# Mixer of a two-layer hybrid encoder on one core: the order of TensorE's products, from the inverses' transposes to w_out, left to a scheduler or written as a list

## The chip, the cores and the metric

One core of a Trainium2 chip. The metric is the device time of one execution in microseconds (us), as the median of several runs; the profile is of one execution more.

## The reference, cut to what matters

Two layers of the following, on 256 tokens of width 1024, all in float32:

```python
x = x + 0.5 * _swiglu(_rmsnorm(x, ffn1_norm[i]), ...)
proj = _rmsnorm(x, mix_norm[i]) @ w_in[i]
q, k, v, z, beta_logit, alpha, hy_in = jnp.split(proj, IN_SPLITS, axis=-1)
o_dn = _deltanet_group(q, k, v, z, beta_logit, alpha, ...)   # both directions
o_hy = _hyena_group(hy_in, ...)                               # two long convolutions
x = x + jnp.concatenate([o_dn, o_hy], axis=-1) @ w_out[i]
x = x + 0.5 * _swiglu(_rmsnorm(x, ffn2_norm[i]), ...)
```

The DeltaNet group is the gated delta rule, run forwards and backwards over the tokens, 4 heads of 128. Per chunk it solves a unit triangular system `a_mat`, then applies the state. The Hyena group takes v, x1, x2 from a short convolution and computes `z = x1 * (conv(v) + skip * v)`, then `z = x2 * (conv(z) + skip * z)`, with long convolutions by Fourier transform, and a norm.

## The kernel before

Activations lie with channels on the partitions (128) and the 256 tokens along the free axis. A large product is a loop over eight blocks of 128 channels. The half steps (SwiGLU) and w_out use weights split in two parts, three products for one; the projections that this change touches use plain float32 weights, 8 products (`pw`) for a chunk of 128 columns, each 128x256 and two instructions long. In this stretch lie the chunks h1 (gate of the first long convolution), v, h2 (gate of the second) and z (the delta rule's gate), four chunks each.

The delta rule's triangular systems, 16 of 128x128 (4 heads, 2 blocks of tokens, 2 directions; four systems make a quarter `q_`), are inverted in place by blocks. VectorE (DVE) makes the 16x16 diagonal blocks into `S`. Then, quarter by quarter: `stp` transposes S into `ST` (ScalarE, ACT, copies it); the step 16 is `pz` (to `zt`, by ACT) and `pp` (subtracted on DVE), 64 columns wide; the steps 32 and 64 are `pzq` (to `zq`, by ACT) and `ppq` (back to S on DVE and to ST on ACT), on 32x32 and 64x64 tiles of the array. Then the solve: `ph` products of S, ST, Mf and Mb with the right-hand sides `rho` (v's transposes `pv`, scaled), scaled to `uf`, `gv` or copied to `ub`; `po` is the output, normed to `on`, transposed back (`pot`), gated to `og`.

The Hyena side: `long_conv` makes `ze` and `zo` (even and odd part of a transform, ACT copies zo to `zq`), ten element-wise operations on DVE and GpSimd, and the inverse transform `py` (512 columns; for the second convolution `py2`, 128 columns). `pt` are h1's transposes to tokens. `acc` are w_out's 192 products, 24 for each of its eight row blocks: four of the Hyena half (blocks 4 to 7, from `yn`), four of the delta rule's (0 to 3, from `og`).

All engines take their instructions from queues in a fixed order. Before, a scheduler sets it at build time, by readiness in its own model and by priorities: each `stage(...)` (lvl, v, h1, quad, lc1, h2, z, hn, hw, solve, o, ow) raises its instructions by an offset. No order is written. PE's instructions thus mix: the delta rule's steps, which wait for each other through ACT and DVE, have pw, py and acc products between. PSUM tiles are two to each of the tags a, b, c, d, so a product waits for the reader of the tile before last.

Of the kernel before, what the change touches and what calls it, by code (L numbers as in the profile page):

```python
# [10 lines left out]
F32 = mybir.dt.float32  # L11
# [62 lines left out]
 'hold': 3,  # L74
 'ej': 0,
# [14 lines left out]
def trunk_kernel(ctx: ExitStack, tc: tile.TileContext, xt, ffn, wba, win, wout, par, fpar, fwo, fnorm, con, feat, wnd, out):  # L90
# [25 lines left out]

    def mm(o, l, r, start=True, stop=True, **kw):
        PE.matmul(o, lhsT=l, rhs=r, start=start, stop=stop, **kw)  # L118
# [202 lines left out]
    def proj32(o, w, ys):  # L321
        for k in range(KD):
            mm(o, w[:, k * 128:(k + 1) * 128], ys[k], start=(k == 0), stop=(k == KD - 1))
# [12 lines left out]
    def rank(acc, w, h, first, last):  # L336

        for m in range(KD):
# [168 lines left out]
    def mixer(l, ys, norm, ab, wcols):  # L507
# [100 lines left out]
        for a in range(2):  # L608
            PE.transpose(pba[:, a], bt[:, a * 128:(a + 1) * 128], ident[0:16, 0:16])
# [214 lines left out]
        def acols(t):  # L824
            return t.rearrange("p m (g b c) -> p m g b c", b=2, c=16)[:, :, :, 0]

        def bcols(t):
            return t.rearrange("p m (g b c) -> p m g b c", b=2, c=16)[:, :, :, 1]


        for q_ in range(4):
            qs = slice(4 * q_, 4 * q_ + 4)
            pz = psum("a", "pz", (128, 4, 4, 16))
            sta, sa, sb = acols(ST[:, qs]), S[:, qs], bcols(S[:, qs])
            for h in range(4):
# [35 lines left out]
        gt = tok("gt", 2)  # L871
        to_tokens(h1, gt)
        z1 = tok("zt", 2)
        for p in range(2):
            py = psum("c", "py", (128, CW))
            mm(py, dft(4 + p), u[p][0], stop=False)
            mm(py, dft(6 + p), u[p][1], start=False)
            V.tensor_tensor(out=z1[p], in0=py, in1=gt[p], op=ALU.mult)
        stage("quad")

        for n in (32, 64):
            for q_ in range(4):
                qs = slice(4 * q_, 4 * q_ + 4)
                pz = psum("a", "pzq", (128, 4, n))
                pp = psum("d", "ppq", (128, 4, n))
                zq = mx.tile([128, 4, n], F32, tag=f"zq{n}", name="zq", bufs=(2 if n == 32 else 1))
                for o in range(0, 128, 2 * n):
                    a, b = slice(o, o + n), slice(o + n, o + 2 * n)
                    for h in range(4):
                        mm(pz[b, h], XX[q_][a, h, b], ST[a, 4 * q_ + h, a])  # L890
                    A.activation(out=zq[b], in_=pz[b], func=AF.Copy)
                    if n == 32 or q_ < 2:
                        for h in range(4):
                            mm(pp[a, h], zq[b, h], S[b, 4 * q_ + h, b])
                        V.tensor_scalar(out=S[a, qs, b], in0=pp[a], scalar1=-1.0, scalar2=None, op0=ALU.mult)
                    if n == 32 or q_ >= 2:
                        for h in range(4):
                            mm(pp[b, h], S[b, 4 * q_ + h, b], zq[b, h])
                        A.activation(out=ST[b, qs, a], in_=pp[b], func=AF.Copy, scale=-1.0)

        stage("lc1")
        u = long_conv(z1, ab[1])

        stage("h2")

        x2 = []
        for i in range(4):
            t = ap_.tile([128, T], F32, tag="hc", name="x2", bufs=4)
            hconv(20 + i, 2, i, t)
            x2.append(t)  # L910
        stage("z")

        zs = []
        for i in range(4):
            t = mx.tile([128, T], F32, tag="zs", name="zs", bufs=4)
            chunk(24 + i, t, AF.Silu)
            zs.append(t)

        stage("hn")
        hn = Norm(4, CW, "b")  # L920
        for i in range(4):
            c = slice(i * 128, (i + 1) * 128)
            py = psum("c", "py2", (128, 2, 128))
            for p in range(2):
                mm(py[:, p], u[p][0][:, c], dft(4 + p), stop=False)
                mm(py[:, p], u[p][1][:, c], dft(6 + p), start=False)
            xv = x2[i].rearrange("c (t p) -> c p t", p=2)
            V.tensor_tensor(out=xv, in0=py, in1=xv, op=ALU.mult)
            hn.add(x2[i])
        hn.finish()  # L930

        stage("hw")

        acc = accumulators("ccdd")
        for i in range(4):
            t = ap_.tile([128, T], F32, tag="t1", name="yn", bufs=7)
            V.scalar_tensor_tensor(out=t, in0=x2[i], scalar=P[:, C_HYN + i:C_HYN + i + 1], in1=hn.rb, op0=ALU.mult, op1=ALU.mult)
            if 28 + i not in PRM["split"]:
                rank32(acc, load_raw(wout[l, 4 + i]), t, i == 0, False)
            else:  # L940
                with pr("feedw"):
                    w = load_w(wout[l, 4 + i])
                rank(acc, w, split_act(t, "y", 8), i == 0, False)
# [17 lines left out]
        uf, ub = [None, None], [None, None]  # L961
        gv1 = tt("gv1", rho[1], gbc(1, 1), ALU.mult)
        uf[0] = tt("uf0", heads("a", lambda h: S[:, 0 + h], rho[0]), gbc(0, 0), ALU.mult)
        p = heads("a", lambda h: ST[:, 12 + h], gv1)
        ub[1] = d2("ub1")
        A.activation(out=ub[1], in_=p, func=AF.Copy)
        p = heads("a", lambda h: Mf[:, h], uf[0])
        V.tensor_tensor(out=rho[1], in0=rho[1], in1=p, op=ALU.subtract)
        p = heads("a", lambda h: Mb[:, h], ub[1])
        V.tensor_tensor(out=rho[0], in0=rho[0], in1=p, op=ALU.subtract)  # L970
        gv0 = tt("gv0", rho[0], gbc(0, 1), ALU.mult)
        uf[1] = tt("uf1", heads("a", lambda h: S[:, 4 + h], rho[1]), gbc(1, 0), ALU.mult)
        p = heads("a", lambda h: ST[:, 8 + h], gv0)
        ub[0] = d2("ub0")
        A.activation(out=ub[0], in_=p, func=AF.Copy)

        stage("o")

        on = []
        for i in range(2):  # L980
# [11 lines left out]
            on.append(tt("on", po, bh(f), ALU.mult))  # L992
        stage("ow")
        for h in range(4):
            pt = psum("b", "pot", (128, T))
            for i in range(2):
                PE.transpose(pt[:, i * 128:(i + 1) * 128], on[i][:, h], ident)
            t = ap_.tile([128, T], F32, tag="t1", name="og", bufs=7)
            V.scalar_tensor_tensor(out=t, in0=pt, scalar=P[:, C_DNN:C_DNN + 1], in1=zs[h], op0=ALU.mult, op1=ALU.mult)
            if 32 + h not in PRM["split"]:  # L1000
                rank32(acc, load_raw(wout[l, h]), t, False, h == 3)
# [147 lines left out]
```

## Time and profile before

| | us |
| --- | --- |
| median of 3 runs | 1250.51 (1249.68 to 1251.75) |
| profiled execution | 1253.56 |
| its span, first to last instruction | 1251.8 |
| PE busy in it | 1210.9 |
| DVE busy | 875.5 |
| ACT busy | 588.8 |

The span is what the trace shows; the time of an execution is a little longer. The mean granted clock of PE over the span is 0.982 of full speed. A product's row counts from its start to its end, and products overlap a little, so in a dense run the distance of two starts is the price of the first.

### The profile page before, as it was taken

Reading aid. Unit: us, or ns where it says so; the run is one execution under the profiler, and the core shown is the slowest. Engines: PE = TensorE matmul, PEld = TensorE weight load, DVE = VectorE, ACT = ScalarE, POOL = GpSimd, SP = SyncE. Lnnn points to the kernel's source line nnn. Section 1 sums busy time; section 2 is a strip of 40 time slices with the busy share of each in tenths; the row PEclk is TensorE's granted clock in tenths of the full one; section 3 lists DMA queues with packets and bytes.
Section 4 is the critical chain, followed back from the end, with each engine's and each line's share of the span. In section 5 each row is a group of like instructions: output and inputs, shape, how many; then the busy total and the mean of one; then the engine's idle time right before and its main releaser. Section 6 shows DMA issues by size and latency. Waiting matters only on the chain.

```text
span 1251.8 us, 20519 instructions
## 1 busy us (share of the span) xinstructions
PE 1210.9 (97%) x7908; PEld 1063.9 (85%) x7908; DVE 875.5 (70%) x1483; ACT 588.8 (47%) x1058; POOL 306.8 (25%) x254
## 2 busy tenths in 40 slices
PE   6999989999999999999999999999999999999997
PEld 5888878978779899998888888888887898999996
DVE  6866677659954666667777767776597656766665
ACT  5544455362323445555554445553432334555553
POOL 5122233211221521113221214430202314111111
PEclk9999999999998899999999999999999988999998
DMA  8555667123222445556645556650231414455551
GB/s 292 172 168 192 195 204 228 31 68 101 69 74 96 135 135 188 190 188 204 210 127 188 181 168 210 222 169 16 77 111 51 136 60 143 156 186 188 193 186 53
DMA packets 53913, 186.36 MB, mean 149 GB/s; under 512 B 6157, under 2 KB 7088, under 8 KB 53816
## 3 DMA queue, kind: packets, MB, share of 16 engines
q1 hardware_dynamic: 50156, 179.01, 43.9%
q10 hardware_dynamic: 3660, 6.05, 1.6%
q8 instruction: 62, 1.02, 0.3%
q14 instruction: 35, 0.29, 0.1%
HBM read 183.98 MB, written 1.05 MB: 148 GB/s over the span
## 4 chain that ended last, share of the span: by engine, by line
PE 71%; DVE 13%; DMA 8%; ACT 3%; issue 3%; POOL 1%; DVEq 0%; SPq 0%; ACTq 0%
PE acc L118 18%; PE g L118 15%; PE u L118 14%; PE pw L118 10%; DMA raw<-in_win 6%; DVE wl L182 4%; DMA raw<-in_ffn 2%; PE py L118 1%; ACT wh L179 1%; PE pe L118 1%; PE pp L118 1%; PE ppq L118 1%; PE ph L118 1%; PE st L118 1%; DVE vs L552 1%
## 5 line engine op out<-in xcount | busy, mean ns | idle before, releaser
L182 DVE TENSOR_TENSOR wl<-raw,wh 128x1024 fp32r<-128x1024 f32 (+1 forms) x270 | 341.4, 1267 | 84.8 <-ACT wh L179 81.2
L179 ACT ACTIVATE wh<-raw 128x1024 fp32r<-128x1024 f32 (+1 forms) x270 | 282.1, 1048 | 121.0 <-PE acc L118 76.0
L118 PE MATMUL acc<-hp,wh 128*128 128x256 f32 x1408 | 265.9, 282 | 0.0
L118 PE MATMUL g<-yp,wh 128*128 128x512 f32 x656 | 245.0, 407 | 8.6 <-DVE yp L157 8.6
L118 PE MATMUL u<-yp,wh 128*128 128x512 f32 x656 | 236.0, 395 | 0.5 <-DVE ub L333 0.3
L118 PEld LDWEIGHTS acc<-hp,wh 128*128 128x128 f32 x1408 | 227.4, 190 | 3.6 <-issue 0.8
L368 POOL TENSOR_TENSOR sr<-gb,rb 128x256 f32<-128x256 f32 x88 | 110.4, 1254 | 450.7 <-ACT gb L366 450.7
L118 PE MATMUL acc<-hp,wl 128*128 128x256 f32 x704 | 194.3, 284 | 8.7 <-DVE wl L182 8.7
L118 PE MATMUL u<-yp,wl 128*128 128x256 f32 x656 | 168.9, 278 | 2.9 <-DVE wl L182 2.9
L118 PE MATMUL g<-yp,wl 128*128 128x256 f32 x656 | 171.7, 282 | 0.0
L118 PEld LDWEIGHTS g<-yp,wh 128*128 128x128 f32 x656 | 124.2, 189 | 40.6 <-DVE yp L157 9.7
L118 PE MATMUL pw<-y,raw 128*128 128x256 f32 x640 | 148.6, 381 | 0.0
L118 PEld LDWEIGHTS acc<-hp,wl 128*128 128x128 f32 x704 | 133.3, 190 | 13.0 <-DVE wl L182 11.1
L118 PEld LDWEIGHTS u<-yp,wh 128*128 128x128 f32 x656 | 123.2, 188 | 22.6 <-PE g L118 0.6
L118 PEld LDWEIGHTS pw<-y,raw 128*128 128x128 f32 x640 | 120.1, 190 | 25.9 <-issue 11.5
L118 PEld LDWEIGHTS u<-yp,wl 128*128 128x128 f32 x656 | 122.9, 188 | 11.3 <-DVE wl L182 4.3
L118 PEld LDWEIGHTS g<-yp,wl 128*128 128x128 f32 x656 | 124.6, 191 | 5.2 <-issue 1.4
L182 POOL TENSOR_TENSOR early<-raw,early 128x512 fp32r<-128x512 f32 (+1 forms) x44 | 75.5, 1729 | 93.9 <-ACT early L179 93.9
L332 ACT ACTIVATE gb<-g 128x256 f32<-128x256 f32 x88 | 33.4, 380 | 120.7 <-PE g L118 117.7
L153 DVE TENSOR_TENSOR hp<-ub,hp 128x256 fp32r<-128x256 f32 x88 | 56.8, 645 | 26.8 <-ACT hp L152 26.6
L333 DVE TENSOR_TENSOR gb<-g,gb 128x256 f32<-128x256 f32 x88 | 37.0, 420 | 44.3 <-ACT gb L332 44.3
L333 DVE TENSOR_TENSOR ub<-u,ub 128x256 f32<-128x256 f32 x88 | 37.0, 420 | 38.4 <-ACT ub L332 38.4
(436 smaller groups left out, 1669.8 us busy)
## 6 DMA issues: line engine op xcount, KB each, us to landing
raw<-in_ffn SPq DMA_DIRECT2D x264, 512.0 KB, 3.9
raw<-in_win SPq DMA_DIRECT2D x56, 512.0 KB, 4.5
raw<-in_wout SPq DMA_DIRECT2D x16, 512.0 KB, 3.9
w<-in_wnd ACTq DMA_DIRECT2D x16, 256.0 KB, 4.4
wo<-in_fwo ACTq DMA_DIRECT2D x8, 130.0 KB
X<-in_xt SPq DMA_DIRECT2D x4, 256.0 KB, 7.5
con_s<-in_con SPq DMA_DIRECT2D x1, 544.0 KB, 9.2
out<-X SPq DMA_DIRECT2D x2, 256.0 KB, 2.5
```

The costliest lines, as they stand in the source:

```text
L118: PE.matmul(o, lhsT=l, rhs=r, start=start, stop=stop, **kw)
L153: eng.tensor_tensor(out=lo, in0=src, in1=hi.bitcast(F32), op=ALU.subtract)
L179: op = A.activation(out=h, in_=raw[:, c], func=AF.Copy)
L182: eng.tensor_tensor(out=l_, in0=raw[:, c], in1=h.bitcast(F32), op=ALU.subtract)
L332: A.activation(out=t, in_=o[:, 1], func=AF.Copy)
L333: V.tensor_tensor(out=t, in0=o[:, 0], in1=t, op=ALU.add)
L368: G.tensor_tensor(out=sr, in0=sg, in1=norm.rb, op=ALU.mult)
L552: i = V.scalar_tensor_tensor(out=dst[:, lo:hi], in0=raw[:, lo + s_:hi + s_], scalar=P[:, w0 + j:w0 + j + 1], in1=dst[:, lo:hi], op0=ALU.mu ...
```

## The change

From `stp` to the last product of w_out, each product and transpose is put behind the one before it on PE (`in_line`: an order without a semaphore, on the same engine). The order is a list in the source: tuples are steps, numbers are gaps, filled with pw products of h2 and z from the generator `bulk()` until the gap's microseconds, at 0.43 a product, are used up. `"h2"` draws products until h2 is done, 99 all that are left. What stands ahead of the list in the source, the chunks of v and h1 and the transposes pv, is not in the line; the scheduler places it. Within the list the priorities are 800 ("delta") and 300 ("hyena").

With it go: all w_out products stand at the end, Hyena's first block, then pot, then the rest; `zq` of the steps 32 and 64 share two buffers (`zqd`), and a step's products for S and ST alternate head by head; pot and all ph use PSUM tag a; the second gate, its norm's sums and the norm are three steps (`py2_`, `st_`, `hn_`). The quarters run as 0, 3, 1, 2.

```diff
+ 'gap_b': 0.4, 'hyena': 300,
+ 'gap_l': 0.9, 'gap_q': 0.5, 'gap_s': 0.6, 'gap_o': 0, 'delta': 800,
...
+    def in_line(i):
+
+        if line[0]:
+            if line[1] is not None:
+                behind(i, line[1])
+            line[1] = i
+
     def mm(o, l, r, start=True, stop=True, **kw):
-        PE.matmul(o, lhsT=l, rhs=r, start=start, stop=stop, **kw)
+        in_line(PE.matmul(o, lhsT=l, rhs=r, start=start, stop=stop, **kw))
...
-        stage("lvl")
-        for q_ in range(4):
-            qs = slice(4 * q_, 4 * q_ + 4)
-            p = psum("a", "stp")
-            for h in range(4):
-                PE.transpose(p[:, h], S[:, 4 * q_ + h], ident)
-            A.activation(out=ST[:, qs], in_=p, func=AF.Copy)
...
+        def stp(q_):
+            p = psum("a", "stp")
+            for h in range(4):
+                transpose(p[:, h], S[:, 4 * q_ + h], ident)
+            A.activation(out=ST[:, quarter(q_)], in_=p, func=AF.Copy)
...
+            for k in range(KD):
+                proj32(p, w, yn, (k,))
+                if k < KD - 1:
+                    yield 0.43
...
+        def lc1_():
+            got["u"] = long_conv(got["z1"], ab[1])
...
+        def bulk():
+            for f_, *a in [(h2_, 0), (h2_, 1), (h2_, 2), (h2_, 3), (z_, 0), (z_, 1), (z_, 2), (z_, 3)]:
+                yield from f_(*a)
...
+        a_, b_, c_, d_ = 0, 3, 1, 2
+        L, Q, W = PRM["gap_l"], PRM["gap_q"], PRM["gap_s"]
+        line[:] = [True, None]
+        rest = bulk()
+        for x in [PRM["gap_b"], (stp, a_), (stp, b_), L, (pz16, a_, 0), (stp, c_), (pz16, b_, 1), (pp16, a_), (stp, d_), (pz16, c_, 0), (pp16, b_),
+                  (pz16, d_, 1), (pp16, c_), (tokens_,), (pzq, 32, a_), (pp16, d_), (pzq, 32, b_), Q, (ppq, 32, a_), (py_, 0), (pzq, 32, c_),
+                  (ppq, 32, b_), (py_, 1), (pzq, 32, d_), (ppq, 32, c_), Q, (pzq, 64, a_), (ppq, 32, d_), 2 * Q, (lc1_,), (pzq, 64, b_), (ppq, 64, a_), Q, (pzq, 64, c_),
+                  (ppq, 64, b_), Q, (fwd, 0), (pzq, 64, d_), (bwd, 1), (ppq, 64, c_), Q, (ppq, 64, d_), W, (less, 1), W, (less, 0), W, (fwd, 1), 2 * W, (bwd, 0), 2 * W,
+                  (po_, 1), (po_, 0), "h2", (py2_, 0), (py2_, 1), (py2_, 2), (py2_, 3), 2 * W, (st_,), 3 * W, (hn_,), 99, (wo_, 4, True), (og_,), (wo_, 5),
+                  (wo_, 6), (wo_, 7), (wo_, 0), (wo_, 1), (wo_, 2), (wo_, 3, False, True)]:
```

What this does to the engines' rows, at three places of layer 0. First PE, from the transposes stp on, before (x8 at stp are two quarters; pw are products of the projections):

```order
L822 MATMUL stp<-con_s,S 128x128 x8
L118 MATMUL pw<-y_2422,raw 128x256 x3
L118 MATMUL zo<-zt,con_s 128x512
L118 MATMUL pw<-y_2417,raw 128x256 x4
L118 MATMUL pw<-y_2422,raw 128x256 x2
L822 MATMUL stp<-con_s,S 128x128 x8
L118 MATMUL pw<-y_2422,raw 128x256 x2
L118 MATMUL pw<-y_2417,raw 128x256
L859 MATMUL pv<-con_s,vs 128x128 x2
L118 MATMUL pw<-y_2417,raw 128x256
L859 MATMUL pv<-con_s,vs 128x128 x2
L118 MATMUL pw<-y_2417,raw 128x256 x2
```

The same place with the change:

```order
L132 MATMUL stp<-con_s,S 128x128 x8
L129 MATMUL zo<-zt,con_s 128x512
L129 MATMUL pw<-y_2417,raw 128x256 x3
L129 MATMUL pz<-ST,xm 128x64 x4
L132 MATMUL stp<-con_s,S 128x128 x4
L132 MATMUL pv<-con_s,vs 128x128 x4
L129 MATMUL pz<-ST,xm 128x64 x4
L129 MATMUL pp<-S,zt_0_79 128x64 x4
L129 MATMUL pp<-zt_0_79,S 128x64 x4
L132 MATMUL stp<-con_s,S 128x128 x4
L129 MATMUL pz<-ST,xm 128x64 x4
```

The pw products between stp and the first pz became three, pz follows at once, and the four transposes pv stand in one group between the second stp and the second pz.

Second, ACT at the same place, before (raw and h are the evacuation and the middle tap of the last h1 chunk):

```order
L823 ACTIVATE ST<-stp 128x512 x2
L530 ACTIVATE raw__3355<-pw 128x256
L540 ACTIVATE h_3351<-raw__3355,par_s 128x256
L470 ACTIVATE zq<-zo 128x512
L853 ACTIVATE vs<-vs 128x256 x4
L823 ACTIVATE ST<-stp 128x512 x2
```

And with the change:

```order
L544 ACTIVATE raw__3263<-pw 128x256
L554 ACTIVATE h_3259<-raw__3263,par_s 128x256
L873 ACTIVATE ST<-stp 128x512 x2
L484 ACTIVATE zq<-zo 128x512
L837 ACTIVATE vs<-vs 128x256 x4
L882 ACTIVATE zt_0_79<-pz 128x16x16
```

The last h1 chunk's copy now stands ahead of the two copies to ST instead of behind them.

Third, PE where the steps of 32 begin, before (py is the inverse transform of the first long convolution; ze begins the second):

```order
L118 MATMUL pzq<-ST,xf 32x32 x4
L118 MATMUL pp<-S,zt_1_80 128x64
L118 MATMUL pp<-zt_1_80,S 128x64 x4
L118 MATMUL py<-t,con_s 128x512
L118 MATMUL py<-ab,con_s 128x512
L118 MATMUL ze<-zt,con_s 128x512
L118 MATMUL pw<-y_2422,raw 128x256 x2
L118 MATMUL ppq<-S,zq 32x32 x4
```

And with the change (the rows of ppq alternate from here, sixteen in all, and the first py stands behind them):

```order
L132 MATMUL pt<-con_s,h_3259 128x128
L129 MATMUL pzq<-ST,xf 32x32 x8
L129 MATMUL pp<-S,zt_1_80 128x64 x4
L129 MATMUL pp<-zt_1_80,S 128x64 x4
L129 MATMUL pzq<-ST,ex 32x32 x8
L129 MATMUL pw<-y_2422,raw 128x256 x2
L129 MATMUL ppq<-S,zqd 32x32
L129 MATMUL ppq<-zqd,S 32x32
```

The py products, which stood ahead of the first ppq, now come behind it, and two pw products stand between pzq and ppq.

## Rows read from the trace of the kernel before

**Rows 1.** The page: busy us of each engine, share, instructions.
```profile
PE 1210.9 (97%) x7908; PEld 1063.9 (85%) x7908; DVE 875.5 (70%) x1483; ACT 588.8 (47%) x1058; POOL 306.8 (25%) x254
```

**Rows 2.** What PE waits for: us, times, longest.
```profile
PE pot L997 <- DVE on L955: 2.4, 2, 1.3
...
PE zo L118 <- DVE zq L476: 1.3, 2, 0.6
...
PE acc L118 <- ACT yp L152: 1.2, 2, 0.7
...
PE pt L572 <- DVE rho L861: 1.1, 2, 0.5
...
PE acc L118 <- DVE yp L153: 1.0, 2, 0.6
...
PE ppq L118 <- ACT zq L891: 0.9, 2, 0.5
...
PE pot L997 <- DVE og L999: 0.9, 2, 0.5
```

**Rows 3.** Window, layer 0's stretch: PE, PEld, DVE, ACT, POOL busy, PEclk, DMA.
```profile
313.20:434.70 121.50, 117.17 (x889) 101.50 (x887) 81.66 (x136) 42.74 (x91) 33.84 (x23) 0.93 0.29 96
```

**Rows 4.** Timeline, PE, layer 0: start, duration, count.
```profile
334.08 1.06 PE L118 MATMUL pp<-zt,S 128*128 128x64 f32 x8
...
336.76 1.95 PE L118 MATMUL pz<-ST,xm 128*128 128x64 f32 x16
...
339.06 1.02 PE L118 MATMUL py<-er,con_s 128*128 128x512 f32 x2
...
342.60 0.43 PE L118 MATMUL pzq<-ST,xf 32*32 32x32 f32 x8
...
348.55 2.02 PE L118 MATMUL py<-t,con_s 128*128 128x512 f32 x2
...
358.70 0.69 PE L118 MATMUL ppq<-zq,S 32*32 32x32 f32 x16
...
359.32 1.12 PE L118 MATMUL ze<-zt,con_s 128*128 128x512 f32 x2
```

**Rows 5.** Windows of layer 0, columns as in rows 3.
```profile
333.30:338.50 5.20, 5.20 (x49) 5.20 (x48) 5.17 (x8) 0.38 (x1) 1.78 (x1) 1.00 0.33 101
...
344.20:347.50 3.30, 3.30 (x39) 3.08 (x39) 0.75 (x2) 0.63 (x3) 0.00 (x0) 1.00 0.00 0
...
347.60:351.00 3.40, 3.40 (x9) 2.07 (x9) 0.75 (x2) 0.00 (x0) 0.00 (x0) 0.50 0.00 0
...
385.20:388.50 3.30, 2.83 (x42) 2.56 (x38) 0.94 (x3) 1.70 (x5) 0.72 (x1) 1.00 0.03 5
...
388.60:395.30 6.70, 6.70 (x37) 6.24 (x38) 2.38 (x7) 1.95 (x6) 0.71 (x1) 0.50 0.00 0
...
415.80:419.20 3.40, 1.59 (x9) 0.69 (x7) 2.35 (x4) 2.10 (x3) 0.59 (x1) 1.00 0.80 280
...
419.30:426.00 6.70, 5.97 (x26) 5.68 (x27) 6.70 (x7) 2.94 (x8) 6.70 (x4) 0.50 0.56 172
```

**Rows 6.** Timeline, PE, around the first transposes of layer 0.
```profile
314.08 2.32 PE L118 MATMUL pw<-y,raw 128*128 128x256 f32 x10
...
316.24 1.04 PE L822 MATMUL stp<-con_s,S 128*128 128x128 f32 x8
...
319.21 1.12 PE L118 MATMUL zo<-zt,con_s 128*128 128x512 f32 x2 [0.64 <-DVE zq L476]
```

**Rows 7.** Timeline, ACT, the same place.
```profile
321.22 0.38 ACT L530 ACTIVATE raw__3355<-pw 128x256 f32<-128x256 f32 x1 [3.27 <-DVE h L552]
...
321.64 0.60 ACT L540 ACTIVATE h<-raw__3355,par_s 128x256 f32<-128x256 f32 x1
...
324.32 1.60 ACT L853 ACTIVATE vs<-vs 128x256 f32<-128x256 f32 x4 [1.60 <-DVE vs L552]
```

**Rows 8.** Timeline, DVE, the last tap of vs.
```profile
325.00 0.47 DVE L552 SCALAR_TENSOR_TENSOR vs<-raw__3270,par_s,vs 128x254 f32<-128x254 f32 x1
```

More of the change, by code (lines that the diff above doesn't have):

```diff
@@ L319, in load_raw, with proj32 @@
         return raw
-    def proj32(o, w, ys):
-        for k in range(KD):
+    def proj32(o, w, ys, ks=range(KD)):
+        for k in ks:
             mm(o, w[:, k * 128:(k + 1) * 128], ys[k], start=(k == 0), stop=(k == KD - 1))
@@ L334, in joined, with rank @@
         return t
-    def rank(acc, w, h, first, last):
-        for m in range(KD):
+    def rank(acc, w, h, first, last, ms=range(KD)):
+        for m in ms:
             for i, (a, b) in enumerate(((0, 0), (1, 0), (0, 1))):
@@ L870, in mixer @@
             h1.append(t)
[L871 to L943, printed above, removed]
@@ new lines, in pz16, with pp16 @@
+        def pz16(q_, n):
+            sta = acols(ST[:, quarter(q_)])
+            pz = psum("a", "pz", (128, 4, 4, 16))
+            for h in range(4):
+                mm(pz[:, h], xm[q_][:, h], sta[:, h])
+            zts[q_] = zt16[n % 2]
+            A.activation(out=acols(zts[q_]), in_=pz, func=AF.Copy)
+        def pp16(q_):
+            qs = quarter(q_)
+            sta, sa, sb, zt = acols(ST[:, qs]), S[:, qs], bcols(S[:, qs]), zts[q_]
+            pp = psum("d", "pp", (128, 2, 4, 4, 16))
+            for h in range(4):
+                mm(pp[:, 0, h], zt[:, h], sb[:, h])
+            for h in range(4):
+                mm(pp[:, 1, h], sa[:, h], acols(zt)[:, h])
+            V.tensor_tensor(out=sb, in0=sb, in1=pp[:, 0], op=ALU.subtract)
+            V.tensor_tensor(out=sta, in0=sta, in1=pp[:, 1], op=ALU.subtract)
@@ new lines, in halves, with pzq @@
+        def halves(n):
+            return [(slice(o, o + n), slice(o + n, o + 2 * n)) for o in range(0, 128, 2 * n)]
+        def pzq(n, q_):
+            pz = psum("a", "pzq", (128, 4, n))
+            zq = zqs[q_] = mx.tile([128, 256], F32, tag="zq", name="zqd", bufs=2)[:, 0:4 * n].rearrange("p (h c) -> p h c", h=4)
+            for a, b in halves(n):
+                for h in range(4):
+                    mm(pz[b, h], XX[q_][a, h, b], ST[a, 4 * q_ + h, a])
+            for a, b in halves(n):
+                A.activation(out=zq[b], in_=pz[b], func=AF.Copy)
@@ new lines, in ppq @@
+        def ppq(n, q_):
+            pp = psum("d", "ppq", (128, 4, n))
+            zq, qs = zqs[q_], quarter(q_)
+            to_s, to_st = n == 32 or q_ < 2, n == 32 or q_ >= 2
+            for a, b in halves(n):
+                for h in range(4):
+                    if to_s:
+                        mm(pp[a, h], zq[b, h], S[b, 4 * q_ + h, b])
+                    if to_st:
+                        mm(pp[b, h], S[b, 4 * q_ + h, b], zq[b, h])
+            for a, b in halves(n):
+                if to_s:
+                    V.tensor_scalar(out=S[a, qs, b], in0=pp[a], scalar1=-1.0, scalar2=None, op0=ALU.mult)
+                if to_st:
+                    A.activation(out=ST[b, qs, a], in_=pp[b], func=AF.Copy, scale=-1.0)
@@ L959, in gbc, with fwd, bwd, less @@
             return bh(gam[:, a, d])
[L961 to L980, printed above, removed]
+        uf, ub, on = [None, None], [None, None], [None, None]
+        def fwd(j):
+            uf[j] = tt("uf", heads(lambda h: S[:, 4 * j + h], rho[j]), gbc(j, 0), ALU.mult)
+        def bwd(j, g_):
+            p = heads(lambda h: ST[:, 8 + 4 * j + h], g_)
+            ub[j] = d2("ub")
+            A.activation(out=ub[j], in_=p, func=AF.Copy)
+        def less(j, M, u_):
+            p = heads(lambda h: M[:, h], u_)
+            V.tensor_tensor(out=rho[j], in0=rho[j], in1=p, op=ALU.subtract)
+        def po_(i):
             po = psum("a", "po")
@@ L991, in mixer @@
             f = rsqrt(ss, 4, f"of{i}")
[L992 to L1001, printed above, removed]
-            else:
-                with pr("feedw"):
-                    w = load_w(wout[l, h])
-                rank(acc, w, split_act(t, "y", 8), False, h == 3)
+            on[i] = tt("on", po, bh(f), ALU.mult)
@@ new lines, in mixer, with chunk_ @@
+        zs, x2, got = [], [], {}
+        def chunk_(c, dst, func=AF.Copy):
+            with pr("feed"):
+                w = load_w(win[l, c]) if c in PRM["split"] else load_raw(win[l, c])
+            p = psum("b", "pw", (128, T))
+            for k in range(KD):
+                proj32(p, w, yn, (k,))
+                if k < KD - 1:
+                    yield 0.43
+            with pr("evac"):
+                i = A.activation(out=dst, in_=p, func=func)
+                if func != AF.Copy:
+                    after(i, last_exp)
+            yield 0.43
@@ new lines, in py_, with py2_ @@
+        def py_(p):
+            py = psum("c", "py", (128, CW))
+            mm(py, dft(4 + p), u[p][0], stop=False)
+            mm(py, dft(6 + p), u[p][1], start=False)
+            V.tensor_tensor(out=got["z1"][p], in0=py, in1=got["gt"][p], op=ALU.mult)
+        def lc1_():
+            got["u"] = long_conv(got["z1"], ab[1])
+        def py2_(i):
+            if i == 0:
+                got["hn"] = Norm(4, CW, "b")
+            u_ = got["u"]
+            c = slice(i * 128, (i + 1) * 128)
+            py = psum("c", "py2", (128, 2, 128))
+            for p in range(2):
+                mm(py[:, p], u_[p][0][:, c], dft(4 + p), stop=False)
+                mm(py[:, p], u_[p][1][:, c], dft(6 + p), start=False)
+            xv = x2[i].rearrange("c (t p) -> c p t", p=2)
+            V.tensor_tensor(out=xv, in0=py, in1=xv, op=ALU.mult)
@@ new lines, in st_, with hn_, og_ @@
+        def st_():
+            for i in range(4):
+                got["hn"].add(x2[i])
+        def hn_():
+            got["hn"].finish()
+            for i in range(4):
+                t = ap_.tile([128, T], F32, tag="t1", name="yn", bufs=7)
+                V.scalar_tensor_tensor(out=t, in0=x2[i], scalar=P[:, C_HYN + i:C_HYN + i + 1], in1=got["hn"].rb, op0=ALU.mult, op1=ALU.mult)
+                got["y", 4 + i] = split_act(t, "y", 8)
+        def og_():
+            for h in range(4):
+                pt = psum("a", "pot", (128, T))
+                for i in range(2):
+                    transpose(pt[:, i * 128:(i + 1) * 128], on[i][:, h], ident)
+                t = ap_.tile([128, T], F32, tag="t1", name="og", bufs=7)
+                V.scalar_tensor_tensor(out=t, in0=pt, scalar=P[:, C_DNN:C_DNN + 1], in1=zs[h], op0=ALU.mult, op1=ALU.mult)
+                got["y", h] = split_act(t, "y", 8)
@@ new lines, in wo_, with gv @@
+        def wo_(i, first=False, last=False):
+            if first:
+                got["acc"] = accumulators("ccdd")
+            with pr("feedw"):
+                w = load_w(wout[l, i])
+            rank(got["acc"], w, got["y", i], first, last)
+        def bulk():
+            for f_, *a in [(h2_, 0), (h2_, 1), (h2_, 2), (h2_, 3), (z_, 0), (z_, 1), (z_, 2), (z_, 3)]:
+                yield from f_(*a)
+        def gv(i):
+            return tt(f"gv{i}", rho[i], gbc(i, 1), ALU.mult)
+        a_, b_, c_, d_ = 0, 3, 1, 2
@@ new lines, in mixer @@
+        L, Q, W = PRM["gap_l"], PRM["gap_q"], PRM["gap_s"]
[7 more added lines that the diff above has]
+                  (wo_, 6), (wo_, 7), (wo_, 0), (wo_, 1), (wo_, 2), (wo_, 3, False, True)]:
+            if isinstance(x, tuple):
+                with pr("delta" if x[0] in (stp, pz16, pp16, pzq, ppq, fwd, bwd, less, po_) else "hyena"):
+                    if x[0] is bwd:
+                        bwd(x[1], gv(x[1]))
+                    elif x[0] is less:
+                        less(x[1], *((Mf, uf[0]) if x[1] else (Mb, ub[1])))
+                    else:
+                        x[0](*x[1:])
+            elif x == "h2":
+                while len(x2) < 4:
+                    next(rest)
+            else:
+                while x > 0:
+                    x -= next(rest, 99)
@@ L1006, in mixer @@
+        acc = got["acc"]
+        line[:] = [False, None]
         stage("ef")
```

57 lines of the change are left out of this document (31 added, 26 removed).

## The prediction

> **What bounds the kernel now.** I began with the busy times of the page. TensorE (PE) is busy for 1210.9 of 1251.8 us, and VectorE (DVE), the next, for 875.5 [rows 1]. So an edit pays only where it shortens PE's work, takes a wait out of PE, or changes the speed at which PE runs. The change touches one stretch in each layer, from the first product of the first long convolution (ze) to the last product of w_out. In layer 0 it lasts from 313.2 to 434.7, 121.5 us [rows 3], of which I count 121.4 from first start to last end; layer 1 has the same stretch 614 us later.
>
> Next I asked what PE waits for in that stretch. The list of its waits counts both layers together: zo 1.3, pt 1.1, ppq 0.9, pot 2.4 and 0.9, acc 1.2 and 1.0, in sum 8.8, so 4.4 us a layer [rows 2]. That is all that a better order could take out of waits.
>
> The third view is the stretch cut into windows. The mean granted clock over it is 0.93 [rows 3], and the row for layer 1 reads alike. The clock has two levels here, 1.0 (2.4 GHz) and 0.50 (1.2 GHz), so 0.07 / 0.5 = 14% of 121.5 us, 17 us a layer, is run at the low one. Work takes twice as long there: two instructions of py take 2.02 instead of 1.02 us [rows 4]. 17 us at half speed lose 8.5 us a layer. **This is the largest price in the stretch, twice all waits**, so the question is where the clock falls and returns under the new order.
>
> What stands ahead of each fall [rows 5]: (a) from 344.20 PE is busy all the time with 64-column pp products and 32x32 pzq, and at 347.6 the level is 0.50; (b) from 385.20 it runs 64x64 steps and short sums, and at 388.6 it falls; (c) from 415.80 it is busy for 1.59 of 3.40 us, with the transposes pot, and falls at 419.3. By contrast the level held from 333.30 to 338.50, all 64-column pp and pz without a pause. So it is not busy time alone: small tiles, transposes and pauses bring the clock down. What stands ahead of each return: 512-column py products (low from 347.6 to 351), a run of 128-column rbp and ph (low 388.6 to 395.3, the first half of it mixed with 64x64 steps and without effect), and w_out products (low 419.3 to 426, the first half with pauses, 5.97 busy of 6.70, and without effect). No return follows a mix of small tiles.
>
> **The change part by part.** *Removed.* The four waits that go with the old places of w_out and of the small steps, and the low pieces (b) and (c), whose causes move. If everything went, a layer's stretch would be 121.4 - 4.4 - 8.5 = 108.5 us of PE work at the full level. No product is added or dropped, so this is the base. The written order visits the 32 and 64 tiles a few times less often. The two instructions of a ze behind such a visit took 1.12 instead of the 1.02 us of their shape [rows 4], so the gain is some tenths a layer, left out of the sum.
>
> *The start of the list, where the order is worse.* In before 17 products of the projections (pw, about 0.22 us an instruction, two for a product) stand between the transposes stp and the first pz; after has 3 and then the first pz. PE's rows give the walk [rows 6]: nine pw products from 314.08 (ten instructions, five of them, take 2.16 to the next row's start) to about 317.97, two stp groups (0.43 each) to 318.84, zo, which waits for DVE until 319.2 as now [rows 6], to 320.2, three pw to 321.4. Then pz of quarter 0 needs ST, a copy on ScalarE (ACT). In the new ACT order the copy of the last h1 projection stands ahead of the two ST copies. It waits for DVE until 321.22 and takes 0.38, its h 0.60 [rows 7]; ST's two copies take 1.09, so pz starts at 322.8. It and one stp end at 324.1. Then the transposes pv stand in PE's row, and behind them everything of the line. They need the four silus of vs, the first at 324.32, 1.60 in all [rows 7], which need DVE's taps, the last from 325.00 to 325.47 [rows 8]. DVE has no pause and the same order there, so pv can't end before about 326.5. Of the 7.7 us from 318.8 to 326.5 PE then works 3.9 (zo 1.0, pw 1.3, pz 0.86, transposes 0.75) and waits **3.8 us**. The last 5.1 us hold 1.7 us of work, pz and transposes only: less than (c), which fell.
>
> *The middle.* Other waits that I expect, estimated from the same chains: the h1 transposes 0.5; the second long convolution, whose zo waits for zq as now, 1.4 for its two pairs; bwd(1) for gv1 on DVE 1.5; fwd(1) for rho 2.4, both behind the ten products of the long convolution on DVE. 5.8 us; with the start **9.6 us**. They lie between nothing (PE is late, so operands are early) and 9.6. I keep 9.6 because the hole is its larger part.
>
> *The clock.* I expect a fall at about 325 to 327. What follows at pv's end, at the full level, by starts of rows [rows 4] (two instructions make a product): a pz quarter 0.87 to 0.98 (two quarters are one row, 1.95 with the drain of its last), a pp quarter 1.75 (sixteen instructions; three rows of eight from 334.08 to 336.76, 0.89 each, 0.84 at best), a pzq quarter 0.72 (two rows of eight, 0.43 with the drain, 0.36 without), a ppq quarter 1.24 (two of 0.62), a py 1.72 (four instructions; a row of two is 1.02 with the drain, 0.86 to the next start), stp 0.43 (half of the row of two groups, 1.04 with the drain [rows 6]). Up to the first py (py_0) the list has three pz 2.6, four pp 7.0, one stp 0.43, twelve transposes 1.3, two pzq 1.44, two pw 0.86, one ppq 1.24 and py_0 1.72: **16.6 us**. A further pzq, ppq and py_1: 3.7, so **20.3**; from there through the last steps of 32 up to the long convolution lc1: 5.9, so **26.2**. In that stretch dense products of 128 columns and more are 0.86 and the two py; everything else is 64 columns, 32x32, 64x64 or transposes, the company in which the level fell or stayed low [rows 5]. A single py at the low level lasts 3.4 us, as long as the low piece that py alone ended (347.6 to 351), but with ppq directly ahead and pzq behind. So I take the return with py_1, and 19.7 us lost (20.3 less the 0.6 that runs at the full level before the fall). The bounds are 16.6 (py_0 does it) and 26.2 (only lc1 does it), and 3 more if the clock falls again in the 64x64 steps behind lc1.
>
> One rule of the Trainium skill bears on this ("TensorE: Matmul & The Clock Gate", Part 4: PE-mode transpose): a transpose on TensorE doesn't count as busy for the clock as a matmul does, so the high level does not engage by it. Our (c), a fall at 419.3 behind transposes and pauses, agrees; by the rule the 1.7 us of transposes among the 64-column steps are gaps too, which makes the return behind py likelier, and were they counted as matmuls, it would be the second rival below, 1257.
>
> *The end.* The 192 products of w_out now stand behind everything, with the transposes pot behind the first 24. That has no hole where before had one, and is in the 108.5. Whether the weights of the following half come in time there I can't see in this trace: 0 to 3 us a layer, taken as 0, since the queue of SP is not held by the line.
>
> **Sum.** 108.5 + 9.6 + 19.7 = 137.8 us a layer against 121.4: +16.4. Two layers: +32.8. The profiled execution (1253.56, span 1251.8) becomes 1286.4. It lies 3.05 above the median of the runs, 1250.51; on that scale it is **1283 us**.
>
> **The rivals.**
> *The clock never falls (faster).* It takes one mechanism: the hole before pv is filled or short, because PE comes later or pv's silus earlier than my walk says. Then the price is waits alone: 108.5 + 9.6 - 121.4 = -3.3 a layer, 1244 us; with the hole filled, too, -7.1 a layer, 1236. For it: the stretch of pure 64-column products that held [rows 5]. Against it: the silus are bound by DVE, whose taps don't move. It decides from a hole of under about 2 us between 321 and 327.
> *The clock falls and returns early, by 64-column work.* Pure pp and pz might bring it back, since they held it. Then 3 to 8 us are lost a layer instead of 19.7; with -3.3 this is -0.3 to +4.7 a layer, 1250 to 1260, middle 1257. Break-even is at 3.3 us lost, a return at about 331. Against it: stp, pv, pt and pzq stand between the pp and pz, and the mix of (a) fell.
> *The low level lasts to lc1 and comes again.* 26.2 - 0.6 + 3 = 28.6 lost, +25.3 a layer, 1301. The waits would shrink under it, so less: 1295.
> *No effect.* The stretch would be bound by DVE either way. Against it: DVE is busy for 81.7 of its 121.5 us [rows 3].
>
> **How the numbers follow.** The low level lasts to the py products or to lc1: 0.74 (this is the forecast and the third rival; its own range is 1268 to 1300: the low end if the 32x32 steps, bound by their issue, slow by half only and the waits vanish). Returns early: 0.10, of which a fifth below 1248, two fifths within 0.2%. Never falls: 0.16, all faster. 0.2% is 2.5 us, about what this kernel's measurement can tell from no change. So faster 0.18, same 0.04, slower 0.78. The range leaves out a part of either end: 1242 to 1299, since the faster case (1236 to 1244) holds too much to be cut off whole.
>
> **What the profile after would show.** PE's row before pv: two pauses, <-ACT ST and <-ACT vs, together over 3 us at about 321 to 326. The granted clock at 0.50 from about 327 until a py (about 350 to 360), and in layer 1 the same, 614 us later. The pieces at 388 and 419 gone, and w_out at the end without a pause. Waits for gv and rho of 1 to 3 us around the solve, less if PE is late. Wrong: a clock of 1.0 through pp and pz, or pv that doesn't wait.

## The result, and the profile after

The changed kernel takes 1279.33 us (median of 5 runs, 1275.48 to 1282.06); the kernel before, 1249.87 us over its 5 runs. The ratio is 1.0223, with a 95% interval of 1.0204 to 1.0242: slower, by 29.5 us. Forecast were 1283 us and 1242 to 1299.

The profiled execution of the change has a span of 1280.2 us (28.4 more). First the page's busy times, which answer to [rows 1]: the span grew by 28.4 us and PE's busy time by 24.2, though no product was added.

```profile
PE 1235.1 (96%) x7908; PEld 1079.2 (84%) x7908; DVE 874.3 (68%) x1483; ACT 589.3 (46%) x1058; POOL 300.3 (23%) x254
```

Where PE got slower is seen in windows of layer 0 (columns as in [rows 3]). The first row is the whole stretch, from ze to the last acc; the next five are its parts, cut where the clock changes:

```profile
313.30:447.80 134.50, 127.38 (x889) 107.27 (x887) 78.01 (x134) 41.66 (x87) 25.76 (x19) 0.84 0.24 77
317.00:327.30 10.30, 7.92 (x44) 5.58 (x42) 10.30 (x26) 4.82 (x11) 0.11 (x1) 1.00 0.15 52
327.40:361.70 34.30, 34.04 (x224) 27.18 (x223) 16.18 (x27) 5.62 (x16) 6.90 (x5) 0.50 0.00 1
361.70:378.00 16.30, 14.11 (x163) 9.51 (x162) 9.46 (x17) 5.57 (x15) 3.53 (x3) 1.00 0.11 33
378.00:388.60 10.60, 9.30 (x39) 7.68 (x40) 8.25 (x12) 1.96 (x4) 3.69 (x3) 0.54 0.16 51
388.60:447.80 59.20, 58.20 (x409) 54.34 (x408) 30.07 (x49) 22.70 (x39) 11.43 (x9) 1.00 0.43 137
```

The stretch went from 121.5 us at a mean clock of 0.93 [rows 3] to 134.5 at 0.84. Two low pieces, 34 and about 10 us, stand where before had three of 3.4, 6.7 and 6.7 [rows 5]; the two late ones of before, at 388.6 and 419.3, are gone from their places. The second piece of the change stands behind 64x64 steps, as the one at 388.6 did. Layer 1 shows the same.

The timeline of PE at the start of the list, which answers to [rows 6], shows what stands ahead of the first fall:

```profile
318.05 1.04 PE L132 MATMUL stp<-con_s,S 128*128 128x128 f32 x8
319.26 1.13 PE L129 MATMUL zo<-zt,con_s 128*128 128x512 f32 x2 [0.18 <-DVE zq L490]
320.23 1.46 PE L129 MATMUL pw<-y,raw 128*128 128x256 f32 x6
322.83 1.11 PE L129 MATMUL pz<-ST,xm 128*128 128x64 f32 x8 [1.14 <-ACT ST L873]
323.77 0.61 PE L132 MATMUL stp<-con_s,S 128*128 128x128 f32 x4
324.84 0.72 PE L132 MATMUL pv<-con_s,vs 128*128 128x128 f32 x2 [0.47 <-ACT vs L837]
326.02 0.72 PE L132 MATMUL pv<-con_s,vs 128*128 128x128 f32 x2 [0.46 <-ACT vs L837]
326.69 1.11 PE L129 MATMUL pz<-ST,xm 128*128 128x64 f32 x8
327.63 1.85 PE L129 MATMUL pp<-S,zt 128*128 128x64 f32 x8
```

The last row is the first at the low level: eight pp take 1.85 instead of 1.06 us [rows 4]. Ahead of it PE waits for ACT's copy ST and for the silus of vs. ACT's timeline gives the reason for the first wait (the answer to [rows 7]): the copies ST start at 322.20, behind the last h1 copy, which waited for DVE until 321.28.

```profile
321.28 0.38 ACT L544 ACTIVATE raw__3263<-pw 128x256 f32<-128x256 f32 x1 [6.75 <-DVE h L566]
321.69 0.60 ACT L554 ACTIVATE h<-raw__3263,par_s 128x256 f32<-128x256 f32 x1
322.20 1.06 ACT L873 ACTIVATE ST<-stp 128x512 f32<-128x512 f32 x2
```

The second piece has its own pause ahead of it (PE's timeline; the ph is bwd(1)): 64x64 steps, 2.48 us of waiting for gv, and then eight ph at half speed.

```profile
376.15 0.68 PE L129 MATMUL pzq<-ST,ex 64*64 64x64 f32 x8
379.30 2.05 PE L129 MATMUL ph<-gv,ST 128*128 128x128 f32 x8 [2.48 <-DVE gv L932]
```

### The profile page after: what moved, and what is told of

It reads as the page before. It is cut to its first block, busy times and chain, and to the rows that moved or that the text cites. A ratio compares the mean times of both kernels' runs of the same rounds, so it can differ in the third digit from the quotient of the medians.

```text
span 1280.2 us, 20513 instructions
## 1 busy us (share of the span) xinstructions
PE 1235.1 (96%) x7908; PEld 1079.2 (84%) x7908; DVE 874.3 (68%) x1483; ACT 589.3 (46%) x1058; POOL 300.3 (23%) x254
## 4 chain that ended last, share of the span: by engine, by line
PE 70%; DVE 13%; DMA 9%; ACT 4%; issue 3%; POOL 1%; SPq 0%; DVEq 0%; ACTq 0%
PE acc L129 16%; PE u L129 14%; PE g L129 14%; PE pw L129 11%; DMA raw<-in_win 6%; DVE wl L196 4%; DMA raw<-in_ffn 3%; PE pp L129 2%; ACT wh L193 1%; PE pe L129 1%; PE py L129 1%; PE ph L129 1%; PE st L129 1%; ACT early L193 1%; DVE vs L566 1%
## 5 line engine op out<-in xcount | busy, mean ns | idle before, releaser
L196 DVE TENSOR_TENSOR wl<-raw,wh 128x1024 fp32r<-128x1024 f32 (+1 forms) x270 | 350.1, 1298 | 97.0 <-ACT wh L193 94.0
L129 PE MATMUL acc<-hp,wh 128*128 128x256 f32 x1408 | 268.9, 285 | 0.1
L129 PE MATMUL pw<-y,raw 128*128 128x256 f32 x640 | 156.2, 393 | 0.0
L129 PEld LDWEIGHTS u<-yp,wl 128*128 128x128 f32 x656 | 123.0, 188 | 10.2 <-DVE wl L196 3.3
```

What stands on the lines that cost most here:

```text
L129: in_line(PE.matmul(o, lhsT=l, rhs=r, start=start, stop=stop, **kw))
L196: eng.tensor_tensor(out=l_, in0=raw[:, c], in1=h.bitcast(F32), op=ALU.subtract)
```

## The experiments

Ten kernels. Their "before" is the kernel before on the same chip, whose median was 1252.3 to 1254.0 us there, 2 to 4 us above the runs that the expectations start from.

**e1_fill_pv: the first pause filled.**

```diff
- 'gap_l': 0.9,
+ 'gap_l': 4.4,
...
-        for a in range(2):
+        def pv_(a):
...
-(pp16, a_), (stp, d_), (pz16, c_, 0), (pp16, b_),
+(pp16, a_), (pv_, 0), (stp, d_), (pz16, c_, 0), (pp16, b_), (pv_, 1),
```

> The gap ahead of the first pz goes from 0.9 to 4.4 us (eight products of h2 move there from the end of the list), and pv's two groups become steps of the line, behind the first and the second pp. Nothing is added or left out. Theory A (the pause ahead of pv makes the clock fall, and the 64-column work can't bring it back): the first low piece, 34 us in each layer, goes or begins only where PE, now early, waits for DVE's subtractions about 333 to 337; 17 us less a layer and 2 of waits, so 1241 to 1250 us; if it falls there all the same, half of it, 1262. Theory B (the mix of 64-column products and transposes brings the clock down whatever stands ahead): a fall within 4 to 8 us of the first pp, 1265 to 1276. Theory C (the clock is not what costs; the order's waits are): 1273 to 1277, the filled pause alone.

1266.36 us, ratio 1.0118 (1.0091 to 1.0145), 13 us below the change. PE's timeline and the windows:

```profile
329.63 1.00 PE L129 MATMUL pz<-ST,xm 128*128 128x64 f32 x8
330.47 1.06 PE L129 MATMUL pp<-S,zt 128*128 128x64 f32 x8
...
337.15 1.14 PE L129 MATMUL pp<-S,zt 128*128 128x64 f32 x8 [3.44 <-DVE ST L894]
338.08 1.92 PE L129 MATMUL pp<-zt,S 128*128 128x64 f32 x8
```
```profile
337.70:358.30 20.60, 20.60 (x161) 14.06 (x160) 6.63 (x16) 4.25 (x13) 1.27 (x1) 0.51 0.00 1
```

The mix of stp, pz, pp and pv that ran at half speed now runs at full speed from 324 to 333 (eight pp in 1.06). Theory B, that the mix alone brings the clock down, falls at this place (e8, below, has another). The clock falls at 338, behind the next pause, 3.44 us for DVE, since PE is now early: A's second branch, 1262, and 4 us above it. This piece is 20.6 us in layer 0 and 17 us in layer 1.

**e2_gv: the second pause taken out.**

```diff
-2 * Q, (lc1_,),
+2 * Q, (gv1_,), (lc1_,),
...
-                        bwd(x[1], gv(x[1]))
+                        bwd(x[1], got["gv1"] if x[1] else gv(x[1]))
```

> gv1, one DVE operation of 0.7 us, is computed ahead of the second long convolution instead of behind its first operations. All else as in the change. It takes the wait of 2.48 us ahead of bwd(1) out. Theory A: the second low piece (10.3 us a layer, 5 lost) goes with it: 2.5 + 5 a layer, 1264 us. Theory B (64x64 steps alone bring the clock down): the fall stays, 1274. Theory C (DVE's chain is the bound, so another product waits instead): 1277 to 1281.

1267.88 us, 1.0126 (1.0098 to 1.0155): 11 us below the change, nearly what A said. From 356.2 on layer 0 has no low piece any more, with the same 64x64 steps in the same order:

```profile
325.60:356.20 30.60, 30.34 (x177) 25.93 (x176) 15.85 (x26) 4.78 (x13) 7.11 (x5) 0.50 0.00 1
356.20:439.50 83.30, 79.98 (x661) 69.27 (x660) 48.42 (x79) 31.31 (x62) 19.25 (x14) 1.00 0.35 111
```

The first piece, of which nothing was changed, is 30.6 us here and 38 us in layer 1 of the same execution. The level returns behind py_0 in layer 0 and only with py_1 in layer 1.

**e4_more: both, and six products ahead of the third pp**, where e1 had to wait.

```diff
-(pz16, d_, 1), (pp16, c_),
+(pz16, d_, 1), 2.5, (pp16, c_),
```

> e1 and e2 together, and six more products (2.6 us) ahead of the third pp, where PE would be ahead of DVE. Theory A: both low pieces go or shrink to a few us, 22 a layer and 4 of waits: 1228 to 1240 us, below the kernel before. Theory B: 1260. Theory C: 1272 to 1278.

1239.05 us, 0.9900 (0.9873 to 0.9926): below the kernel before. The whole stretch runs at the full level in both layers (layer 0, and the place where e1 waited 3.44 us):

```profile
312.30:426.10 113.80, 106.56 (x889) 91.54 (x888) 77.19 (x135) 41.75 (x88) 27.45 (x19) 1.00 0.28 91
```
```profile
337.14 1.08 PE L129 MATMUL pp<-S,zt 128*128 128x64 f32 x8 [0.80 <-DVE ST L894]
```

So PE's work in the stretch, all 889 instructions at the full level, is 106.6 us.

**e5_nogap: e4 without those six products**, so one number of the list differs.

> e4 without its six products ahead of the third pp: only that gap is taken out, they go to the end of the list. Theory A (a pause while small work runs makes the clock fall): PE waits for DVE's subtraction ahead of the third pp as in e1 (3.4 us), the clock falls at about 338 and returns near 358, 20 us low, 10 lost and 2.6 more of waits a layer against e4, 1251 to 1264 us. Theory B' (what holds the clock in e4 is gv's place and the start alone): 1239 to 1242.

1254.08 us, 1.0008 (0.9988 to 1.0027); single runs from 1247.7 to 1259.1. The wait is back, and so is the low level:

```profile
336.97 1.44 PE L129 MATMUL pp<-S,zt 128*128 128x64 f32 x8 [3.45 <-DVE ST L894]
```
```profile
337.70:354.40 16.70, 16.70 (x147) 12.69 (x148) 6.52 (x15) 3.18 (x9) 1.27 (x1) 0.50 0.00 1
```

The level returns behind py_0, and layer 1 is low for as long. In e4 the same place waits 0.8 us and keeps the level. Six products, which only moved, are worth about 14 us (the medians differ by 15.0, the ratios to the kernel before on each chip by 1.1%).

**e6_return: a run of dense products inside the low piece of the change.**

```diff
-(pz16, c_, 0), (pp16, b_),
+(pz16, c_, 0), (pp16, b_), 3.5,
```

> The change with one gap more: nine products (3.9 us at the full level) behind the second pp, in the midst of the first low piece; they go missing at the end of the list. Theory A (the low level ends with products of 128 columns and more in a run, not with time): the clock returns in or right behind this gap, at about 341 to 345 instead of 361.7, 8 to 10 us less a layer, 1259 to 1264; if DVE then makes PE wait and it falls again, 1265 to 1275. Rival (it ends by the py products or at a set time): the return stays at about 362, 1279.

1257.90 us, 1.0042 (1.0025 to 1.0058): 21 us below the change, a little more than A said, since the second low piece, still there at 375.7, is shorter too (6.8 us, not 10.2). The nine products take 5.98 us, the first part of them at half speed; the level is back at 341.4 instead of 361.7, and pp behind them takes 1.06 again:

```profile
336.77 1.06 PE L132 MATMUL pv<-con_s,vs 128*128 128x128 f32 x4
337.62 5.98 PE L129 MATMUL pw<-y,raw 128*128 128x256 f32 x18
343.44 1.00 PE L129 MATMUL pz<-ST,xm 128*128 128x64 f32 x8
344.28 1.06 PE L129 MATMUL pp<-S,zt 128*128 128x64 f32 x8
```
```profile
324.30:341.40 17.10, 16.66 (x68) 15.41 (x69) 14.49 (x22) 3.05 (x8) 6.19 (x5) 0.50 0.01 1
341.60:375.70 34.10, 30.59 (x361) 22.53 (x360) 16.84 (x33) 11.86 (x33) 5.19 (x5) 1.00 0.15 48
```

So the low level ends neither at a set time nor only by the py products: here it ended within a run of 128x256 products, and 13 us of 64-column products and transposes ahead of them, with PE 97% busy, had not ended it.

**e3_noline: the new source with the scheduler's order.**

```diff
-        line[:] = [True, None]
+        line[:] = [False, None]
```

> The line is never switched on, so the scheduler orders PE as in before, from the new source: w_out late in the source, zq in two buffers, step products alternating, priorities 800 and 300. Theory A: without the pauses of the written order the clock stays up: 1245 to 1258 us. If the other parts of the change (w_out at the end, the alternation) cost by themselves: 1270 or more.

1265.62 us, 1.0115 (1.0089 to 1.0141). A miss: the written order isn't the whole loss. The windows (the stretch, then its three low pieces):

```profile
312.30:439.60 127.30, 119.08 (x889) 101.07 (x887) 74.27 (x135) 41.76 (x90) 28.83 (x20) 0.92 0.25 81
338.80:342.30 3.50, 3.50 (x5) 1.33 (x6) 1.47 (x4) 0.00 (x0) 0.01 (x1) 0.53 0.00 0
349.30:355.90 6.60, 6.60 (x25) 4.61 (x26) 1.42 (x4) 0.86 (x4) 0.00 (x0) 0.50 0.00 0
376.60:386.60 10.00, 9.47 (x44) 8.03 (x43) 8.35 (x11) 2.42 (x4) 6.46 (x4) 0.50 0.21 76
```

PE idles 8.2 us of the stretch, where before it idled 4.3 [rows 3], and 20 us are at the low level instead of 17. The stretch is 5.8 us longer than before [rows 3], which is nearly all of the 13 us over two layers. So the rest of the new source costs under the scheduler, too; whether by the order that comes of it or by its shared buffers isn't separated here.

**e10_wo: e3 with Hyena's part of w_out written ahead of the rest of the solve**, as in before.

```diff
-(ppq, 64, d_), W, (less, 1), W, (less, 0), W, (fwd, 1), 2 * W, (bwd, 0), 2 * W,
...
+(ppq, 64, d_), "h2", (py2_, 0), (py2_, 1), (py2_, 2), (py2_, 3), (st_,), 99, (hn_,), (wo_, 4, True), (wo_, 5),
+(wo_, 6), (wo_, 7), (less, 1), (less, 0), (fwd, 1), (bwd, 0), (po_, 1), (po_, 0), (og_,), (wo_, 0), (wo_, 1)
...
```

> e3 (line off) with Hyena's half, its norm and its four blocks of w_out written ahead of the second half of the solve, as in before, the delta rule's four blocks last. If what e3 loses against before (13 us) comes of w_out's late place, which leaves the solve without dense products beside it: 1246 to 1253 us. If it comes of the rest of the new source (how the scheduler mixes the steps of 32 and 64): 1260 to 1268.

1280.01 us, 1.0227 (1.0195 to 1.0259): worse, not better. A miss of both branches: writing Hyena's part of w_out early doesn't win back what e3 lost, and costs 14 us more. What in the new source costs e3 its 13 us stays open.

**e7_alt: the kernel before with the alternating products alone.**

```diff
-                    if n == 32 or q_ < 2:
-                        for h in range(4):
+                    for h in range(4):
+                        if to_s:
                             mm(pp[a, h], zq[b, h], S[b, 4 * q_ + h, b])
-                        V.tensor_scalar(out=S[a, qs, b], in0=pp[a], scalar1=-1.0, scalar2=None, op0=ALU.mult)
-                    if n == 32 or q_ >= 2:
-                        for h in range(4):
+                        if to_st:
                             mm(pp[b, h], S[b, 4 * q_ + h, b], zq[b, h])
```

> The kernel before with one part of the change: in the steps 32 and 64 the products for S and for ST alternate head by head, both ahead of the two copies. Nothing else. If alternating products on two tiles of the array run beside each other (a quarter of ppq 0.5 instead of 1.24 us): 2.5 to 3 us less a layer, 1244 to 1247 us. If the scheduler's order or the clock eats it (a fall earlier or later): 1248 to 1256.

1246.09 us, 0.9949 (0.9934 to 0.9964): 6.8 us less. In PE's timeline products for S and for ST start in pairs, at nearly the same time, and the quarter's 32 instructions are over at 371.15, 0.62 us after the first:

```profile
370.53 0.21 PE L118 MATMUL ppq<-S,zq 32*32 32x32 f32 x1
370.54 0.21 PE L118 MATMUL ppq<-zq,S 32*32 32x32 f32 x1
370.58 0.19 PE L118 MATMUL ppq<-S,zq 32*32 32x32 f32 x1
...
371.15 0.91 PE L118 MATMUL pzq<-ST,xf 64*64 64x64 f32 x12
```

The windows of the two layers' stretches show that the gain isn't this alone:

```profile
311.50:431.70 120.20, 113.48 (x889) 97.22 (x887) 78.83 (x136) 42.02 (x91) 33.13 (x23) 0.94 0.30 95
921.80:1039.80 118.00, 111.42 (x889) 95.81 (x887) 78.88 (x135) 41.99 (x91) 33.16 (x23) 0.96 0.29 95
```

Without what the clock took (0.06 of 120.2 and 0.04 of 118.0 us) PE's work is 106.3 to 106.7 us, as in e4, and in before by the same count 108.7 (117.17 less 0.07 of 121.5, [rows 3]): some 2 us less a layer, 4 of the 7 us. A few us of low clock went as well, and 2.4 us of idle time came.

**e8_tuned: e4 with eight products at three of its waits.**

```diff
-(pz16, d_, 1), 2.5, (pp16, c_),
+(pz16, d_, 1), 3.4, (pp16, c_),
...
-(fwd, 1), 2 * W, (bwd, 0),
+(fwd, 1), 2.1, (bwd, 0),
...
-(py2_, 0), (py2_, 1), (py2_, 2),
+(py2_, 0), (py2_, 1), 1.6, (py2_, 2),
```

> e4 with products at three more of its waits: two more ahead of the third pp (0.8 us of waiting left), two more ahead of bwd(0) (0.9), four ahead of the third py2 (1.67); five are left for the end of the list. If the waits are on the path: 2.5 to 3.4 us less a layer, 1232 to 1234 us. If they only move (the norm's chain is then uncovered): 1237 to 1240.

1234.57 us, 0.9858 (0.9843 to 0.9872), the fastest here, 18 us below the kernel before. Layer 1's stretch is 111.3 us without a low piece; layer 0's has one of 6.8 us, in the last of these windows:

```profile
337.88 0.74 PE L132 MATMUL pt<-con_s,h 128*128 128x128 f32 x4 [0.49 <-DVE rho L846]
```
```profile
333.00:337.00 4.00, 4.00 (x29) 3.51 (x28) 4.00 (x9) 0.38 (x1) 0.36 (x1) 1.00 0.39 131
337.00:340.70 3.70, 3.21 (x39) 2.86 (x37) 3.67 (x9) 2.71 (x6) 0.91 (x1) 1.00 0.02 4
340.70:347.50 6.80, 6.80 (x59) 4.26 (x59) 1.41 (x5) 1.07 (x4) 0.00 (x0) 0.50 0.00 0
```

This fall has no long pause ahead of it: PE works for 7.21 of the 7.70 us up to it, and its one wait there is 0.49 us. The products from 334.9 on are pp, transposes pt and pzq. It is like the first fall of the kernel before, at 347.6, behind 64-column products and 32x32 tiles with no pause at all [rows 5]. So a pause is one way to lose the level; a run of narrow products can lose it without one, though in e4 nearly the same run kept it. What decides between the two stays open.

**e9_pt: e8 with two products behind h1's transposes**, ahead of that piece.

```diff
-(pp16, c_), (tokens_,), (pzq, 32, a_),
+(pp16, c_), (tokens_,), 0.8, (pzq, 32, a_),
```

> e8 with two more products (0.8 us) between h1's transposes and the first pzq, where layer 0 of e8 had a low piece of 6.5 us from 341. Theory A: the piece goes, 3 us: 1231 to 1233 us. If the products are missed at the end of the list, where three are left: 1234 to 1236.

1235.32 us, 0.9865 (0.9842 to 0.9888): no gain that can be measured over e8, and not A's 1231 to 1233. The piece is gone in the profiled execution, and the stretch is 111.6 us. But e8 didn't show the piece in layer 1, and its profiled execution has a mean clock of 0.993, the other three 0.995, so most of them need not have had it. That the two products took it away isn't shown.

## Why the prediction was right

*The bound.* PE, and by its clock: shown. Between e5 and e4 one gap of six products moves, no work is added, and the low piece and about 14 us go. A bound by DVE would have left the time (theory C in e1 and e2, which fell).

*The walk at the start.* Forecast: zo at 319.2, pz at 322.8, pv's end about 326.5, a fall at 325 to 327. Measured: 319.26, 322.83, 326.7, 327.6. The places came from DVE's and ACT's rows of before: DVE's order didn't change there, and ACT's only by the h1 copy. The idle time in it was over-counted: 2.25 us in PE's row (0.18, 1.14, 0.47, 0.46), 2.4 of the 10.3 us of the window from 317.0, not 3.8; the pauses for ST and vs come to 2.07, not to over 3. It was enough all the same. The mark that the prediction gave to its first rival, a hole of under about 2 us, has no row behind it: e8 falls behind a wait of 0.49. That the pause brought it is shown by e1, where the same mix without it ran at the full level.

*How long the level stays low.* I took the return with py_1 and 19.7 us lost. It came with py_1, at 361.7, in both layers. That it was py_1 has luck in it: e2, whose list is the same up to there, has it behind py_0 in one layer and with py_1 in the other. e6 shows the step behind it: a run of wide products brings the level back. The price was too high. Half of the 34.3 us would be 17.1, but the 32x32 products don't take twice as long at the low level, which the prediction had as a condition of its low end. Sixteen pzq in the change and in e4:

```profile
349.51 0.87 PE L129 MATMUL pzq<-ST,ex 32*32 32x32 f32 x16
```
```profile
343.23 0.59 PE L129 MATMUL pzq<-ST,ex 32*32 32x32 f32 x16
```

The sum below leaves some 16 us for this piece. Of the 4 that are missing, 1.2 are the two ppq quarters ahead of py_1, which are shorter with alternating products: 0.62 us each by e7, not the 1.24 that I took from before.

*The second fall.* I had it as a bound, 0 to 3 us lost; about 10 us at half speed make it 5. The base had taken the piece behind the 64x64 steps out, as one whose cause moves; it moved with them. Its cause was on my list as a wait (bwd(1) for gv, 1.5 us; measured 2.48) and not as a fall. e2 takes the wait out and the fall goes.

*The sum.* Forecast for a layer: 108.5 of work, 9.6 of waits, 19.7 of clock, 137.8. Measured in layer 0: 134.5 long and 7.1 idle, from the window; 106.6 of work, from e4's window; so 20.8 for the clock, some 16 in the first piece and 5 in the second. Work and waits were too high by 1.9 and 2.5, the clock too low by 1.1. So the close total is in part luck: the first piece was priced 4 too high, and the second, 5, stood in no term. The 108.5 missed the alternation, which stands in the change's description and got no price; by e7 it is worth about 2 us, all of the 1.9. Of the waits, the 2.4 of fwd(1) for rho, for which the prediction showed no row, didn't come.

*What the forecast had wrong in kind.* It charged everything to the written order. e3 shows that with the order left out 13 us of the loss against before stay; the list itself costs about 14 us more than the scheduler with the same source. The two halves need not be the same microseconds, since e3's low pieces and waits lie in other places.

*The rivals.* That the clock never falls was the faster side, 1236 to 1244, with the hole filled: e4 and e8 are that case, made on purpose, at 1239 and 1235. That 64-column work brings the level back early: not seen; 17 us of it in the change, from 327.6 to the first pzq at 345, with hardly a pause, didn't. The prediction's reading that small tiles, transposes and pauses bring the clock down holds for the pauses by e1, e2 and e5; for narrow products without a long pause there are both cases, a fall in e8 and none in e4.

*Weighed against the trace.* The Trainium skill ("TensorE: Matmul & The Clock Gate", Part 4: PE-mode transpose) says that a transpose doesn't count as busy for the clock as a matmul does. The fall behind pv's and stp's transposes agrees. By itself that isn't enough here: in e4 the same transposes stand among the same products at 1.0.

## What to carry to other kernels

Where TensorE is the bound, read its granted clock in windows before its waits: here pauses of 2 to 3.5 us among narrow products cost 5 to 16 us each, since the engine ran at the low level until wide products came in a run. Narrow products without such a pause are no guarantee either (e8, layer 0). A hand-written order is good only where its fillers stand at the waits; look in the other engines' rows for when each operand can be ready, put the spare products there, and look again, since an engine that is no longer late meets the next wait. A change of several parts can hide the gain of one: the alternation by itself made the kernel before 7 us faster, some 4 of them in PE's work.

## What the runs showed of the hardware that I had not expected

Products of 32 rows and columns on two different tiles, issued in turn, start at nearly the same time (370.53 and 370.54 in e7); 32 instructions of a ppq quarter took 0.62 us, as long as 16 did before (358.70 to 359.32 in [rows 4]).

The time of one program varies from run to run, at its ends with the mean clock: the change's five runs go from 1275.48 to 1282.06 us at mean clocks of 0.965 and 0.959, and e5's ten from 1247.7 at 0.986 to 1259.11 at 0.978. e8, which holds the level nearly throughout, stays within 1234.10 to 1234.74. A program that falls needs more runs.
